# Four of the Mamba layer's x blocks formed by seven block products, with the convolution moved behind a round trip through DRAM

## The chip, the core and the metric

The kernel runs on one core of a Trainium2 chip. The metric is device microseconds of one execution, the median of three runs. The chip's engines are named as in the profile: PE (matrix products), PEld (its weight loads), DVE (vector), ACT (scalar), POOL (general purpose) and SP, which here issues DMAs.

## The reference

Two layers of a decoder over 256 tokens of width 2048 in float32: a latent attention mixer with a squared-ReLU MLP, then a Mamba-2 mixer with another MLP. Only the Mamba mixer changes:

```python
zxbcdt = h @ w_in                      # 2048 -> 4096 (z) + 4096 (x) + 1024 (b) + 1024 (c) + 64 (dt)
z, xbc, dt = jnp.split(zxbcdt, [SSM_D_INNER, SSM_D_INNER + SSM_CONV_DIM], axis=-1)
xbc = jax.nn.silu(causal_depthwise_conv(xbc, conv_w, conv_b))      # 4 taps along the tokens
xs, b_in, c_in = jnp.split(xbc, [SSM_D_INNER, SSM_D_INNER + SSM_GROUPS * SSM_STATE], axis=-1)
...
dt = jax.nn.softplus(dt.astype(jnp.float32) + dt_bias.astype(jnp.float32))
...
y = ssd_chunked_scan(xs, dt, a, b_in, c_in)    # one chunk of 256 tokens, 64 heads in 8 groups
y = y + d_skip * xs
y = y.reshape(B, S, SSM_D_INNER) * jax.nn.silu(z)
y = group_rms_norm(y) * norm_g                 # written out in the reference
return y @ w_out
```

## The kernel before

**Products.** Every float32 operand is split into a rounded part (`wh`, on ACT, L102) and the rest (`wl`, on DVE, L103). A product is three matmuls: rounded by rounded, rest by rounded, rounded by rest. Weights come in *units* of 128 partitions by 1024 floats (512 KB): two slices of depth 128 by 512 output columns. A plain unit is 12 matmuls (2 slices, 2 halves of the tokens, 3 each). `Flow` holds one fixed list of units for the whole run. `next` hands PE the unit at hand, has the splits of the next three put into the program, and the loads of up to six more. `raw` has 6 buffers, `wh` and `wl` 4 each, so a split can be at most four units ahead of PE.

**Order.** PE runs in the order in which the program is written. The other engines are ordered when the kernel is built: among what is ready, the earlier written comes first. After each key of a `block` (two units, 24 matmuls) `tick` is called, a *step*; `later(n, fn)` writes out `fn` at the step after n more. `pump` writes one or two heads of the scan per step. `behind("last_load")` and its like set an instruction behind the last load, split or `wh` written so far.

**The Mamba stage.** `SSM_ORDER` (L1408) names the blocks of 512 columns: B0, d (dt), C0, x0, B1, x1, C1, x2, z0 and so on, then the output blocks o0 to o3. What surrounds the change:

- `bc_block`: four keys, then `conv` in two halves, one step apart: PE transposes, 12 operations of DVE over a few columns each (L1122), tanh, and a last product (L1125).
- `dt_block`: one narrow product (L358), at a later step `fold` (L366) and `dt_chain`, some 20 small DVE operations that mostly wait on one another (L1151 to L1167); three steps later `cums` (L1173) on PE, one step later `back`.
- `x_block`: four keys, ACT copies the two results into `xt` (L1223) and writes them to DRAM (`xD`). Two steps later `shift` reads three shifted copies back (`taps`, L1231) on SP's queue. Then DVE does the four taps: `mult` (L1238, 3072 columns), `some` (L1241, L1243), `total` (L1247); ACT the tanh, DVE `silu` (L1254). `ahead` puts the group's eight heads into `pump`'s list and starts `across` (L1268).
- `head`: `cm` by DMA, four small ACT operations, a score product on DVE for four heads (L1306); after eight heads `products` (L1318) on PE.
- `z_block`: four keys, the gate once the group is ready (L1357 to L1363), transposes two steps later. `o_block`s follow when their groups are gated.

**Seven products in the MLP.** The MLP already forms pairs of 512-column blocks by a Winograd form of Strassen's scheme. The operand is cut in two by tokens and in two by depth, the weights in two by depth and in two by columns. `seven` (L170) gives the seven weight combinations, named M1, N7, N5, N6, N4, M2, N3, each in four depths d, and each a unit that PE uses for one half of the tokens only (6 matmuls). N7, N5 and N6 need an addition on DVE (L183) before their split, N4 an accumulating DMA from POOL (L199) after N6. `combinations` forms the token sums once (L528 to L538), and a planner, `merged`, weaves the units with plain ones so that DVE's work stays near a set share of PE's time.

## Time and profile before

| | us |
|---|---|
| median of 3 runs | 2287.03 (2286.62 to 2288.36) |
| the profiled execution | 2286.11 |
| its span, first to last instruction | 2284.3 |
| first matmul of B0 | 948.53 into the span |
| last output pair of the stage begins its second half (o3) | 1561.38 |
| the second MLP's first matmul | 1607.26 |

The profile is of one execution. In a view of groups a row gives line, engine, operation, output and input, shape and count, then busy time and mean ns of one, then the idle time of the engine just ahead of them. A row of waits reads: who waited for whom, total us, times, longest. The mean of one instruction includes its overlap with the next; distances between starts tell what a run of them costs.

### The profile page before, as it was taken

The numbers are of one execution on the slowest core, as the hardware profiler recorded it, in microseconds if no ns is written. First come the engines' busy times: TensorE is split into PE (matmuls) and PEld (weight loads), VectorE is DVE, ScalarE is ACT, GpSimd is POOL, SyncE is SP. The second block draws the span as 40 slices with busy tenths as digits, with TensorE's granted clock in tenths as the row PEclk, the third lists the DMA queues.
The fourth block names the chain that finished last, engine by engine and source line by source line (L and its number), as shares of the span: only waits on it lengthen the run. The fifth ranks groups of instructions, "written<-read, shape, count | busy, mean of one in ns | idle before, by whom it ended". The sixth has DMA issues, their size and how long they took to land.

```text
span 2284.3 us, 30685 instructions
## 1 busy us (share of the span) xinstructions
PE 2277.1 (100%) x10929; PEld 1889.3 (83%) x10929; DVE 1895.8 (83%) x2167; ACT 1407.8 (62%) x2006; POOL 268.0 (12%) x315
## 2 busy tenths in 40 slices
PE   9999999999999999999999999999999999999999
PEld 7898888888888888888888888888888888888887
DVE  7786697999898897677888678666989889989985
ACT  6775475666566666575666655545666666666663
POOL 1440000000000000100133212111000000000000
PEclk9999999999999999999999999999999999999999
DMA  8545678888888878667888878767688888888874
GB/s 315 173 153 153 215 229 263 260 259 271 263 253 260 270 231 271 228 191 262 275 278 280 254 255 279 228 217 228 205 259 250 263 269 254 259 275 249 265 233 160
DMA packets 167705, 557.16 MB, mean 244 GB/s; under 512 B 19040, under 2 KB 28192, under 8 KB 166528
## 3 DMA queue, kind: packets, MB, share of 16 engines
q1 hardware_dynamic: 151264, 502.44, 66.7%
q0 software_dynamic: 13888, 48.49, 10.1%
q10 hardware_dynamic: 2400, 4.27, 0.5%
q8 instruction: 86, 1.41, 0.2%
q14 instruction: 67, 0.55, 0.1%
HBM read 529.65 MB, written 6.41 MB: 235 GB/s over the span
## 4 chain that ended last, share of the span: by engine, by line
PE 97%; DMA 1%; DVE 1%; ACT 1%; issue 0%; POOL 0%; SPq 0%; ACTq 0%; DVEq 0%
PE acc L339 13%; PE acc L340 13%; PE acc L343 13%; PE yp L616 9%; PE yp L617 9%; PE yp L618 9%; PE st L617 7%; PE st L618 7%; PE st L616 7%; PE sm L324 1%; PE y L1318 1%; PE sm L322 1%; PE acc L617 1%; PE acc L618 1%; PE acc L616 1%; DMA wraw<-mi 1%
## 5 line engine op out<-in xcount | busy, mean ns | idle before, releaser
L102 ACT ACTIVATE wh<-wraw 128x1024 fp32r<-128x1024 f32 (+1 forms) x818 | 857.1, 1053 | 572.2 <-PE acc L340 263.0
L103 DVE TENSOR_TENSOR wl<-wraw,wh 128x1024 fp32r<-128x1024 f32 (+1 forms) x818 | 991.8, 1228 | 235.5 <-ACT wh L102 225.6
L616 PE MATMUL yp<-wh,k 128*128 128x512 f32 x896 | 349.2, 390 | 0.0
L618 PE MATMUL yp<-wh,k 128*128 128x512 f32 x896 | 348.8, 389 | 0.0
L617 PE MATMUL yp<-wl,k 128*128 128x512 f32 x896 | 348.6, 389 | 0.0
L339 PE MATMUL acc<-wh,xt 128*128 128x512 f32 x704 | 279.6, 397 | 1.1 <-ACT wh L102 1.1
L340 PE MATMUL acc<-wh,xt 128*128 128x512 f32 x704 | 274.6, 390 | 0.2 <-DVE xt L481 0.2
L102 ACT ACTIVATE wh<-wrx 128x1024 fp32r<-128x1024 f32 x168 | 177.8, 1059 | 152.8 <-PE yp L618 96.7
L103 DVE TENSOR_TENSOR wl<-wrx,wh 128x1024 fp32r<-128x1024 f32 x168 | 204.0, 1219 | 35.3 <-ACT wh L102 34.7
L618 PEld LDWEIGHTS yp<-wh,k 128*128 128x128 f32 x896 | 168.2, 188 | 35.2
L616 PEld LDWEIGHTS yp<-wh,k 128*128 128x128 f32 x896 | 168.2, 188 | 34.8
L617 PEld LDWEIGHTS yp<-wl,k 128*128 128x128 f32 x896 | 168.2, 188 | 34.8
L339 PE MATMUL acc<-wh,k 128*128 128x512 f32 x496 | 196.5, 396 | 0.0
L340 PE MATMUL acc<-wh,k 128*128 128x512 f32 x496 | 193.3, 390 | 0.0
L343 PE MATMUL acc<-wl,xt 128*128 128x512 f32 x704 | 188.3, 389 | 0.0
L616 PE MATMUL st<-wh,xt 128*128 128x512 f32 x448 | 177.7, 397 | 0.0
L618 PE MATMUL st<-wh,xt 128*128 128x512 f32 x448 | 174.9, 390 | 0.0
L617 PE MATMUL st<-wl,xt 128*128 128x512 f32 x448 | 174.7, 390 | 0.0
L339 PEld LDWEIGHTS acc<-wh,xt 128*128 128x128 f32 x704 | 132.4, 188 | 30.4 <-ACT wh L102 2.4
L340 PEld LDWEIGHTS acc<-wh,xt 128*128 128x128 f32 x704 | 132.3, 188 | 28.7 <-issue 1.2
L343 PEld LDWEIGHTS acc<-wl,xt 128*128 128x128 f32 x704 | 132.1, 188 | 27.7
L199 POOL DMA_DIRECT2D wrx<-mi x56 | 49.1, 876 | 719.8 <-DVE wl L103 523.7
(323 smaller groups left out, 3505.7 us busy)
## 6 DMA issues: line engine op xcount, KB each, us to landing
wraw<-mi SPq DMA_DIRECT2D x256, 512.0 KB, 5.5
wraw<-mo SPq DMA_DIRECT2D x256, 512.0 KB, 5.4
wraw<-si SPq DMA_DIRECT2D x160, 512.0 KB, 5.1
wraw<-so SPq DMA_DIRECT2D x64, 512.0 KB, 5.1
wrx<-mi SPq DMA_DIRECT2D x56, 512.0 KB, 5.2
wrx<-mi POOLq DMA_DIRECT2D x56, 512.0 KB, 7.6
wraw<-wo SPq DMA_DIRECT2D x32, 512.0 KB, 4.0
taps<-xD SPq DMA_DIRECT2D x16, 768.0 KB, 7.7
```

Source lines behind the costliest of these rows:

```text
L102: self.last = nc.scalar.activation(h[:, v], raw[:, v], AF.Copy)
L103: self.last_lo = nc.vector.tensor_tensor(lo[:, v], raw[:, v], h[:, v].bitcast(F32), ALU.subtract)
L199: nc.gpsimd.dma_start(st["b11"].tile, quarter(d, 1, 0), accum_op=ALU.add)
L322: self.nc.tensor.transpose(b.bitcast(F32R)[:, v], words[:, v], self.ident_r)
L324: self.nc.tensor.transpose(b[:, v], src[:, v], self.ident)
L339: nc.tensor.matmul(accs[t][:, :n], ah, wh[:, q, :], start=first and kt + q == 0, stop=False)
L340: nc.tensor.matmul(accs[t][:, :n], al, wh[:, q, :], start=False, stop=False)
L343: nc.tensor.matmul(accs[t][:, :n], lhs(kt + q, t)[0], wl[:, q, :], start=False, stop=en and q == nk - 1)
L616: nc.tensor.matmul(b, ah, wh, start=first and q == 0, stop=False)
L617: nc.tensor.matmul(b, ah, wl, start=False, stop=False)
L618: nc.tensor.matmul(b, al, wh, start=False, stop=last and q == 1)
L1318: nc.tensor.matmul(y[t][c, o], heads[j // 4][:, t, j % 4, c], xg[g][t][:, o], start=True, stop=True)
```

## The change

The x blocks 0 to 3 are taken out of the plain list and formed as two column pairs by seven products each. A first part runs B0, dt and the two pairs, each woven with two plain blocks (C0 and x4, then x5 and x6). All x results go to DRAM. A second part runs the remaining blocks, and in it `x_conv` (the steps `v0` to `v7`) reads x and its shifted copies back and does the convolution, then the heads as before.

The sums of tokens and the products:

```diff
+    def sums_of_tokens(self, pool):
...
+        def whole(i, t):
+            first = self.flow.pools["rx"] if len(f) < 3 else pool
+            v = first.tile([P, 1024], F32, tag="rx" if len(f) < 3 else "fy", name=self.name("xf"))
...
+            for q in range(2):
+                h, lo = (x[:, :, t * P:(t + 1) * P].bitcast(F32) for x in self.xT[2 * i + q])
+                nc.vector.tensor_tensor(v[:, q * 512:(q + 1) * 512].rearrange("p (k n) -> p k n", n=P), h, lo, ALU.add)
...
+        def one():
+            a21, a11, a22 = whole(0, 1), whole(0, 0), whole(1, 1)
+            sub(a22, a21, a22)
+            put("N5", a22)
...
+    def ssm_seven(self, S, p, filler, out):
...
+            elif name in ("N5", "N6"):
+                if count.get("N5") != 4 or count.get("N6") != 4:
+                    return
+                w, g, e = v["w"], v["g"], v["e"] = [self.scratch() for _ in range(3)]
+                sub(w, bank["N6"], v["m1"])
+                plus(g, bank["N7"], w)
+                plus(e, bank["N5"], g)
+                out(p, 1, 1, e, e)
...
+        for tok in woven(p):
+            if tok[0] != "s":
+                filler(tok)
+                continue
...
+                nc.tensor.matmul(bank[onto], ah, wh, start=done + q == 0 and not skip, stop=False, skip_group_check=skip)
+                nc.tensor.matmul(bank[onto], al, wh, start=False, stop=False, skip_group_check=skip)
+                nc.tensor.matmul(bank[onto], ah, wl, start=False, stop=done == 3 and q == 1, skip_group_check=skip)
+            if done == 3:
+                after(name)
+            self.spend(1.36)
+
+    def spend(self, us):
+        self.spent += us
+        if self.spent >= 5.4:
+            self.spent -= 5.4
+            self.tick()
```

M2 is summed onto M1's bank and N3 onto N5's. In the woven part a step comes when 5.4 us of planned PE time are spent. The convolution:

```diff
+        def put_x(g, t, src, dst):
+            nc.scalar.activation(dst, src, AF.Copy, scale=rs[t])
+            nc.scalar.dma_start(xD[3 + t * P:3 + (t + 1) * P, g * 512:g * 512 + 512], dst)
...
+        def x_conv(g):
+            xt = sp2.tile([P, 2, 512], F32, tag="xtm", name=f"xtm{g}", bufs=4)
...
+            def fetch():
                 with behind("last_load"):
...
+                    nc.sync.dma_start(xt, x_rows(g, 0, 2))
+                    weight(3)
+                    load(2)
+                    weight(2)
+                    load(1)
+                    weight(1)
+                    load(0)
...
+            def tapped(k):
+                nc.vector.tensor_tensor(tap[k], tap[k], both(k), ALU.mult)
+                nc.vector.tensor_tensor(xt, xt, tap[k], ALU.add)
...
             def mult():
...
                 with behind("last_lo"):
...
+                    nc.vector.tensor_tensor(xt, xt, both(3), ALU.mult)
+                    tapped(2)
+                with behind("last_load"):
+                    weight(0)
+                    weight(4)
...
+            self.later(0, fetch)
+            self.later(1, lambda: cb_group(g))
+            self.later(2, mult)
+            self.later(3, lambda: tapped(1))
+            self.later(4, total)
+            self.later(5, lambda: (silu(), ahead()))
```

`load(k)` reads 512 KB of rows shifted by k from `xD` into one of three `tap` tiles, `weight(k)` 256 KB of tap weights into one of three `cw` tiles. The two parts and their order:

```diff
+        with ExitStack() as first:
+            sp1 = first.enter_context(self.tc.tile_pool(name="ssm1", bufs=1, reuse_waits="tile"))
+            self.flow.pools["rx"] = first.enter_context(self.tc.tile_pool(name="rx", bufs=4, reuse_waits="tile"))
+            sums, steps = self.sums_of_tokens(sp1)
+            for n, fn in enumerate(steps):
+                self.later(n, fn)
+            bc_block("B", 0)
+            dt_block()
+            for p in range(2):
+                self.ssm_seven(sums, p, filler, lambda p, j, t, src, dst: put_x(2 * p + j, t, src, dst))
+        sp2 = later.enter_context(self.tc.tile_pool(name="ssm2", bufs=1, reuse_waits="tile"))
+        self.pump = pump
...
-SSM_ORDER = ["B0", "d0", "C0", "x0", "B1", "x1", "C1", "x2", "z0", "x3", "z1", "x4", "z2", "o0", "x5", "z3", "x6", "z4", "o1",
-             "x7", "z5", "z6", "o2a", "z7", "o2b", "o3"]
+SSM_FILLERS = [[("C", 0), ("x", 4)], [("x", 5), ("x", 6)]]
+SSM_ORDER = ["v0", "x7", "B1", "v1", "z0", "v2", "z1", "C1", "v3", "z2", "z3", "v4", "o0a", "v5", "o0b", "z4", "v6",
+             "o1a", "v7", "o1b", "z5", "z6", "o2a", "z7", "o2b", "o3"]
```

`woven(p)` lists the 28 block units and 16 plain units of a pair by a running count of planned PE and DVE time. Written out, the first pair begins C0.0, C0.1, M1, N7, C0.2, N5, C0.3, N6, C0.4, M1, N7, C0.5, C0.6, N5, C0.7 and ends M2 four times, N3 three times, N4, N3, x4.7. The second pair has the same form with x5 and x6. The banks of `conv` and `cb_group` now come from one pool of two (`sm`) alone, since the plain blocks of the woven part hold the other (`yp`). The head and score tiles lie in the second part's pool, the dt tiles in the first's.

## The prediction

> **What bounds the kernel now.** I read the page first: engines, chain, then the waits of PE, then the Mamba stage in windows.

> ```profile
> span 2284.3 us, 30685 instructions
> ...
> PE 2277.1 (100%) x10929; PEld 1889.3 (83%) x10929; DVE 1895.8 (83%) x2167; ACT 1407.8 (62%) x2006; POOL 268.0 (12%) x315
> PE 97%; DMA 1%; DVE 1%; ACT 1%; issue 0%; POOL 0%; SPq 0%; ACTq 0%; DVEq 0%
> ```

> PE is busy for the whole span and the chain that ended last is 97% PE. The waits of PE, complete:

> ```profile
> PE warmed L451 <- DVE warm L448: 1.4, 1, 1.4
> PE acc L339 <- ACT wh L102: 1.1, 1, 1.1
> PE yp L939 <- ACT xt L944: 0.6, 1, 0.6
> PE yp L939 <- DVE qn L887: 0.4, 1, 0.4
> PE acc L340 <- DVE xt L481: 0.2, 1, 0.2
> PE st L617 <- DVE wl L103: 0.2, 1, 0.2
> ```

> 3.9 us in all. So every matmul taken out shortens the run by its issue distance, and every new wait of PE lengthens it in full. The profiled execution took 2286.11 us, 1.8 over its span and 0.9 under the median of 2287.03; the sum is made on 2286.11 and the 0.9 added at the end.

> The windows' columns are stretch, length, then busy time (and instructions) of PE, PEld, DVE, ACT, POOL, then clock, DMA share, GB/s: nearly the whole Mamba stage, the middle of the second MLP, 150 us of x blocks, and 17 us that matter below.

> ```profile
> 950.50:1558.50 608.00, 608.00 (x3179) 501.26 (x3178) 465.81 (x510) 360.28 (x603) 115.66 (x75) 1.00 0.76 249
> 1629.00:2228.00 599.00, 598.83 (x2706) 494.22 (x2705) 545.33 (x533) 383.63 (x413) 37.49 (x52) 1.00 0.84 256
> 1110.00:1260.00 150.00, 150.00 (x888) 123.52 (x887) 131.49 (x128) 100.07 (x191) 52.20 (x29) 1.00 0.84 284
> 981.40:998.40 17.00, 17.00 (x80) 13.87 (x78) 15.52 (x34) 10.39 (x15) 0.00 (x0) 1.00 0.59 182
> ```

> The Mamba stage has DVE at 77% of PE's time, the MLP, which already forms its input product from seven block products, at 91%, both without a PE wait worth naming. The change spends DVE time to save PE time, so the question is whether DVE fits.

> **The saving.** Two ends of weight units on PE (a unit is 12 matmuls: eight with `wh`, four with `wl`):

> ```profile
> 921.10 1.07 PE L343 MATMUL acc<-wl,k 128*128 128x512 f32 x4
> 923.82 1.07 PE L343 MATMUL acc<-wl,k 128*128 128x512 f32 x4
> 887.01 0.40 PE L618 MATMUL st<-wh,xt 128*128 128x512 f32 x1
> 887.70 0.39 PE L618 MATMUL st<-wh,xt 128*128 128x512 f32 x1
> ```

> 923.82 - 921.10 = 2.72 us for 12, 0.227 each; in the MLP's block products three take 0.69, the same pace. Two plain x blocks are 2 x 8 units x 12 = 192 matmuls; seven products of four half units are 28 x 6 = 168. Two pairs save 2 x 24 x 0.227 = **10.9 us**. The transposes, score products and head products keep their counts, and `C0`, `x4`, `x5`, `x6` remain plain. The copies of x out of PSUM stay 16 on ACT; it issues 16 writes instead of 8, on an engine that is 62% busy.

> **What DVE gets.** First the prices: one 1024-column operation, its distance when they follow each other, and the small ones.

> ```profile
> L103 DVE TENSOR_TENSOR wl<-wraw,wh 128x1024 fp32r<-128x1024 f32 x231 | 276.9, 1219 | 26.3 <-ACT wh L102 22.4
> 1628.92 2.35 DVE L103 TENSOR_TENSOR wl<-wraw,wh 128x1024 fp32r<-128x1024 f32 x2
> 1631.19 1.22 DVE L103 TENSOR_TENSOR wl<-wrx,wh 128x1024 fp32r<-128x1024 f32 x1
> 1590.22 1.28 DVE L300 TENSOR_TENSOR xt<-sm,xt 128x512 fp32r<-128x512 f32 x2
> ```

> Alone 1.22, but two take 1631.19 - 1628.92 = 2.27 in sequence, so 1.14 each; for 512 columns two span 1.28 at 0.68 each, so they start 0.60 apart. A pair by seven products needs, for each of four depths, 2 operations for N7, N5, N6 and 1 for M1, N4, M2, N3: 40 instead of 16. That is 24 x 1.14 + 5 combinations x 0.60 = 30.3, twice 60.6. The sums of tokens add eight additions of 512 columns, four subtractions and four splits: 4.8 + 9.1 = 13.9. The convolution's one product of 3072 columns becomes three of 1024, the same elements, which I cost at nothing; two more starts per group would be under 2 us in all. DVE in the stage goes from 465.8 to 540.3 us, PE from 608 to 597: 90.5%, as in the MLP. On average it fits; by place it does not.

> **First part (B0, dt, two woven pairs).** PE needs 21.8 + 3.8 + 2 x 81.6 = 189 us. DVE: 2 x (56 x 1.14 + 3.0) = 134 for the pairs, 13.9, and 28 for B0, dt, the two halves of B0's and of C0's convolution and the residual: 176, 93%. But most of the extra lies in the first 50 us. The second MLP opens the same way, with its sums beside a plain block, and there DVE is only just in time:

> ```profile
> 1630.23 0.45 PE L617 MATMUL yp<-wl,xt 128*128 128x512 f32 x1
> ```

> The split that started at 1628.92 ended 1.2 us later, about 1630.1, and PE uses it at 1630.23: no lead is left. The Mamba stage adds B0's convolution and the dt chain at just that point. Before, the fold, the chain and the cumulative sums run so (rows of PE's and DVE's timelines, with others left out):

> ```profile
> 981.48 0.56 PE L366 MATMUL sm<-cst,s 128*128 128x64 f32 x4
> 983.62 0.27 DVE L1151 SCALAR_TENSOR_TENSOR dt<-sm,rs,cst 128x64 f32<-128x64 f32 x1
> ...
> 988.63 0.28 DVE L1158 TENSOR_TENSOR dt<-dt 128x128 f32<-128x128 f32 x1
> 988.83 1.22 DVE L103 TENSOR_TENSOR wl<-wraw,wh 128x1024 fp32r<-128x1024 f32 x1
> 990.57 0.22 DVE L1159 TENSOR_SCALAR dt<-dt 128x128 f32<-128x128 f32 x1
> 990.71 1.22 DVE L103 TENSOR_TENSOR wl<-wraw,wh 128x1024 fp32r<-128x1024 f32 x1
> ...
> 996.01 0.36 DVE L1166 SCALAR_TENSOR_TENSOR dt<-dt,aneg 128x64 f32<-128x64 f32 x2
> 998.39 0.65 PE L1173 MATMUL sm<-tri,dt 128*64 128x256 f32 x2
> ```

> The chain of small dependent operations takes 983.62 to 996.37 and is done 2.0 us before PE's fixed order reaches `cums` (L1173). After each dependent step a ready split slips in (L1158, L103, then L1159). In the change `cums` still comes three steps after the fold, 16.3 us of PE: M1, N7, C0.2, N5, C0.3, N6, C0.4, M1, N7. The window from fold to `cums` had DVE busy 15.5 of 17.0 with six splits (6.8 us); the nine units now need 13 operations, 14.8 us. 15.5 + 8.0 = 23.5, which is 6.5 over, and there is no lead to pay from. **PE waits 6.5 us, at `cums` or just ahead of it.** Bounds: were the chain preferred always, a lead of three units (about 4 us) could pay, 2.5; were each of some 15 dependent steps (0.3 us) followed by a 1.14 us operation, the chain takes 22 us after a start 2 us late, 24 against 16.9, plus ACT's part: up to 11. During this wait DVE runs its units ahead, so C0's convolution (6 us over two steps) is covered afterwards: the pairs alone use 67 of 81.6.

> The granted clock is 1.00 in every window above and PE never idles there. [...]

> **Second part (v0 to o3).** DVE has 540 - 176 = 364 us for 455 of PE. The last 26 steps (z5 to o3) hold 52 splits and little else, some 80 us; so the first 50 steps, with all eight convolutions, hold about 285 in 50 x 5.44 + 32 = 304 us: 94%. GpSimd makes DVE slower here:

> ```profile
> L103 DVE TENSOR_TENSOR wl<-wraw,wh 128x1024 fp32r<-128x1024 f32 x49 | 65.8, 1355 | 12.6 <-ACT wh L102 12.6
> wraw<-si SPq DMA_DIRECT2D x160, 512.0 KB, 5.1
> taps<-xD SPq DMA_DIRECT2D x16, 768.0 KB, 7.7
> cw<-cwx SPq DMA_DIRECT2D x8, 1280.0 KB, 8.7
> wrx<-mi POOLq DMA_DIRECT2D x56, 512.0 KB, 7.6
> ```

> (1355 ns in 1110 to 1260 against 1219 in the MLP; that is inside the 465.8.) DMA: 100 units x 0.524 MB, per group four times 0.524 and five times 0.262 MB instead of 1.57 + 1.31, and some 13 MB of head rows, gains and copies: 93 MB in 304 us, 306 GB/s. 284 GB/s took a share of 0.84, so 0.91. The rows read back were not seen in this form: 512 KB lies by size between 5 and 8 us (the first three rows), and `mult` comes two steps, 10.9 us, after `fetch`. They are hidden while the queue is free; without that cover DVE waits, and the 2.9 MB of one `fetch`, 9 us at 338 GB/s, also stand on SP's queue ahead of the next weights, which have some 16 us. SP issues six DMAs more per group. The new pool of this part lies where the sums lay, so the first `fetch` waits for PE's last N3, and x7's later weights stand behind it if SP gets there first. N6's eight accumulating DMAs on POOL land in 7.6 us by the last row, and N4 is planned 12 us after N6, so they are hidden as in the MLP; a late one would hold N4's split and what DVE has behind it. I take **2.5 us** of PE wait for this part, from 0 (like the MLP) to 12 (below).

> **Sum.** 2286.1 - 10.9 + 6.5 + 2.5 = 2284.2, with 0.9 for the median **2285.1 us**.

> **Rivals.** The measurement tells 0.2% (4.6 us) from no change.
> - *DVE keeps up* (32%): the chain is preferred (2.5) and the second part hides all: -8.4, 2278.6; with no loss at all 2276.1. For it: the MLP has 0.2 us of wait at 91%. Against it: the 6.5 over in a window without lead.
> - *DVE and DMA saturate in the second part* (24%): if DVE can be filled only to the MLP's 91%, 285 us of work take 313 instead of 304, +9, and with a few us of weights behind the read-backs +12: 2287.0 - 10.9 + 6.5 + 12 = 2294.6, slower. It decides from about 9 us in the second part. For it: 94% and a DMA share of 0.91, both above any window shown.
> [...]
> - That the change saves nothing has no room: 48 matmuls are gone from PE's list.

> **Chances.** Forecast 36% (2282.5 to 2291.5) and clock gate 8%, both within 0.2%: 44%. DVE keeps up: faster, 32%. Saturation: slower, 24%. The range takes in the first rival but for its last half us, and above it the saturated second part with 2.4 us more of the wait at `cums`, whose bound is 11: 2276.5 to 2297.

> **What would show it.** Right: a PE wait of 3 to 10 us at `cums` (or on a split just ahead) some 50 us after B0 starts, DVE without idle time from B0's start to there, the Mamba stage about 2 us shorter, PE waits in the second part under 5 us. Wrong: no PE wait at `cums` (then 2279), waits on splits spread over v1 to v6 (then 2290 and more), or a granted clock under 1 after a wait.

## The result and the profile after

| | before | after |
|---|---|---|
| median, us | 2286.82 (2286.37 to 2288.36) | 2346.03 (2342.47 to 2352.64, 4 runs) |
| after / before | | 1.0261, 95% interval 1.0237 to 1.0285 |
| span of the profiled execution, us | 2284.3 | 2345.2 |
| matmuls on PE | 10929 | 10881 |
| PE busy, us | 2277.1 | 2292.8 |
| PE not busy within the span, us | 7.2 | 52.4 |

The kernel is 59 us slower; the forecast was 2285.1 with a range to 2297. The page of the changed kernel, span, engines and the chain's shares:

```profile
span 2345.2 us, 30882 instructions
...
PE 2292.8 (98%) x10881; PEld 1895.2 (81%) x10881; DVE 1968.5 (84%) x2257; ACT 1439.3 (61%) x2036; POOL 269.1 (11%) x323
...
PE 33%; DMA 2%; DVE 2%; issue 1%; ACT 1%; SPq 0%; POOL 0%; DVEq 0%; ACTq 0%
```

The 48 matmuls are gone and DVE has 72.7 us more (74.5 were forecast). But the chain that ended last is no longer nearly all PE. The span's 60.9 us come apart in three terms: the saving, -10.9; PE not busy, 52.4 - 7.2 = +45.2; and PE busy for longer with fewer matmuls, 2292.8 - (2277.1 - 10.9) = +26.6. Together 60.9. The seven largest rows of PE's waits in the changed kernel (us in total, times, the longest):

```profile
PE sm L1302 <- DVE s L1225: 10.5, 2, 6.0
PE sm L322 <- DMA tr<-s: 6.6, 4, 4.0
PE sm L1277 <- DVE dt L1270: 6.3, 1, 6.3
PE sm L367 <- DVE s L1225: 4.4, 1, 4.4
PE sm L1216 <- DVE s L1225: 4.3, 1, 4.3
PE sm L1389 <- POOL s L1385: 3.9, 1, 3.9
PE acc L343 <- DVE wl L103: 3.1, 2, 2.0
```

`L1277` is `cums`: 6.3 us, where 6.5 were forecast. But it is one row of many. Three rows, 19.2 us, wait for a bank that `L1225` still reads (`L1302`, `L367`, `L1216`). The others wait for data: `cums` for dt, the transposes of `L322` for words that a DMA brings, `L1389` for a product of POOL. Waits on splits, which were the worry of the prediction, are 5.1 us: `L343` and, further down the list, `L618` with 2.0. In time, from PE's timeline (start, duration, operation, idle time before it and what ended it):

```profile
985.86 1.08 PE L367 MATMUL sm<-cst,s 128*128 128x64 f32 x4 [4.40 <-DVE s L1225]
1012.03 0.66 PE L1277 MATMUL sm<-tri,dt 128*64 128x256 f32 x1 [6.28 <-DVE dt L1270]
1037.41 0.44 PE L1216 MATMUL sm<-ident,s 128*128 128x128 f32 x1 [4.27 <-DVE s L1225]
1232.45 0.77 PE L1302 MATMUL sm<-k,k 128*128 128x256 f32 x1 [5.96 <-DVE s L1225]
1319.91 0.77 PE L1302 MATMUL sm<-k,k 128*128 128x256 f32 x1 [4.51 <-DVE s L1225]
```

Four of these five end when `L1225` ends: the tap operations of `conv`, which add up a half of B's or C's convolution straight out of the PSUM bank. DVE's timeline just ahead of the first of them:

```profile
977.13 0.47 DVE L1225 SCALAR_TENSOR_TENSOR s<-sm,cst,s 128x255 f32<-128x255 f32 x1
977.52 1.21 DVE L103 TENSOR_TENSOR wl<-wraw,wh 128x1024 fp32r<-128x1024 f32 x1
978.66 0.47 DVE L1225 SCALAR_TENSOR_TENSOR s<-sm,cst,s 128x254 f32<-128x254 f32 x1
979.05 1.21 DVE L103 TENSOR_TENSOR wl<-wraw,wh 128x1024 fp32r<-128x1024 f32 x1
980.18 0.47 DVE L1225 SCALAR_TENSOR_TENSOR s<-sm,cst,s 128x253 f32<-128x253 f32 x1
980.57 1.21 DVE L183 TENSOR_TENSOR wrx<-wrx,wraw 128x1024 f32<-128x1024 f32 x1
...
985.24 0.47 DVE L1225 SCALAR_TENSOR_TENSOR s<-sm,cst,s 128x253 f32<-128x253 f32 x1
```

Six operations of 0.47 us, in two chains of three that depend on one another, are 2.8 us of work. They take from 977.13 to 985.71, since a 1.2-us operation goes in after each. The fold (`L367`), next in line for a bank, begins at 985.86, just after the last has read it. PE runs in the order of the program, so everything behind the fold stands for those 4.40 us too. In the kernel before, the same half of B0 (there `L1122`) ran so:

```profile
976.81 1.51 DVE L1122 SCALAR_TENSOR_TENSOR s<-sm,cst,s 128x255 f32<-128x255 f32 x3
...
979.85 1.51 DVE L1122 SCALAR_TENSOR_TENSOR s<-sm,cst,s 128x255 f32<-128x255 f32 x3
```

Three at a time, with one split between the threes: 4.6 us instead of 8.6. And the next half worked on a bank of `yp`, so that `sm` had its second bank free.

The third term is mostly the clock. Windows of the same trace: in the first wait (981.46 to 985.86), from its last 0.8 us on, behind that, then behind a wait of 2.87 us (ended at 1384.82) and behind one of 2.01 us (ended at 1429.76). The column before the last two is the granted clock:

```profile
981.64:985.05 3.41, 0.00 (x0) 0.00 (x0) 3.06 (x5) 0.07 (x1) 0.00 (x0) 1.00 0.88 280
985.05:991.88 6.83, 6.02 (x16) 4.98 (x17) 5.52 (x12) 2.89 (x6) 0.00 (x0) 0.50 0.22 84
991.88:995.29 3.41, 3.41 (x16) 2.75 (x15) 2.79 (x7) 2.46 (x4) 0.00 (x0) 1.00 0.52 159
...
1384.90:1387.90 3.00, 3.00 (x10) 2.52 (x11) 3.00 (x3) 2.75 (x7) 0.00 (x0) 0.51 0.63 249
1429.80:1432.80 3.00, 2.90 (x17) 2.39 (x18) 3.00 (x3) 2.29 (x4) 0.00 (x0) 1.00 0.83 239
```

Behind the waits of 4.40 and 2.87 us the clock is 0.50 or 0.51, behind that of 2.01 us it is 1.00. At 0.50 PE has 16 matmuls in 6.02 us, at 1.00 16 in 3.41. From 987.28 to 991.55 they stand 0.43 us apart instead of 0.227. "Busy" hides this: PE is busy the whole time, only slower. The trace has ten such stretches in the Mamba stage, 54.6 us together, with PE busy for 45.6 of them; at half pace that is some 23 of the 26.6 us. The rest was not followed up.

### The profile page after: what moved, and what is told of

The parts are those of the page before. It is cut to its first block, busy times and chain, and to the rows that moved or that the text cites. A ratio compares the mean times of both kernels' runs of the same rounds, so it can differ in the third digit from the quotient of the medians.

```text
span 2345.2 us, 30882 instructions
## 1 busy us (share of the span) xinstructions
PE 2292.8 (98%) x10881; PEld 1895.2 (81%) x10881; DVE 1968.5 (84%) x2257; ACT 1439.3 (61%) x2036; POOL 269.1 (11%) x323
## 3 DMA queue, kind: packets, MB, share of 16 engines
q10 hardware_dynamic: 2528, 4.27, 0.5%
## 5 line engine op out<-in xcount | busy, mean ns | idle before, releaser
L102 ACT ACTIVATE wh<-wraw 128x1024 fp32r<-128x1024 f32 (+1 forms) x818 | 857.3, 1053 | 535.6 <-PE acc L340 197.6
L103 DVE TENSOR_TENSOR wl<-wraw,wh 128x1024 fp32r<-128x1024 f32 (+1 forms) x818 | 989.2, 1227 | 191.4 <-ACT wh L102 182.3
L617 PE MATMUL yp<-wh,k 128*128 128x512 f32 x896 | 349.3, 390 | 0.0
L618 PE MATMUL yp<-wl,k 128*128 128x512 f32 x896 | 348.6, 389 | 0.0
L102 ACT ACTIVATE wh<-wrx 128x1024 fp32r<-128x1024 f32 x192 | 203.3, 1059 | 177.0 <-PE yp L619 99.1
L103 DVE TENSOR_TENSOR wl<-wrx,wh 128x1024 fp32r<-128x1024 f32 x192 | 233.2, 1220 | 46.3 <-ACT wh L102 45.7
L339 PE MATMUL acc<-wh,k 128*128 128x512 f32 x496 | 197.0, 397 | 0.0
L617 PEld LDWEIGHTS yp<-wh,k 128*128 128x128 f32 x896 | 168.2, 188 | 34.9
L618 PEld LDWEIGHTS yp<-wl,k 128*128 128x128 f32 x896 | 168.2, 188 | 34.9
L340 PE MATMUL acc<-wh,k 128*128 128x512 f32 x496 | 193.9, 391 | 0.0
L339 PE MATMUL acc<-wh,xt 128*128 128x512 f32 x448 | 181.6, 405 | 0.0
L340 PE MATMUL acc<-wh,xt 128*128 128x512 f32 x448 | 178.2, 398 | 0.3 <-DVE xt L482 0.2
L617 PE MATMUL st<-wh,xt 128*128 128x512 f32 x448 | 177.7, 397 | 0.0
L618 PE MATMUL st<-wl,xt 128*128 128x512 f32 x448 | 174.7, 390 | 0.0
L618 PE MATMUL st<-wl,sN 128*128 128x512 f32 x336 | 131.6, 392 | 2.0 <-DVE wl L103 2.0
L617 PE MATMUL st<-wh,sN 128*128 128x512 f32 x336 | 133.1, 396 | 0.0
L343 PE MATMUL acc<-wl,k 128*128 128x512 f32 x496 | 132.7, 389 | 0.0
L619 PE MATMUL st<-wh,sN 128*128 128x512 f32 x336 | 131.1, 390 | 0.0
## 6 DMA issues: line engine op xcount, KB each, us to landing
wraw<-mi SPq DMA_DIRECT2D x256, 512.0 KB, 5.7
wraw<-mo SPq DMA_DIRECT2D x256, 512.0 KB, 5.5
wraw<-si SPq DMA_DIRECT2D x160, 512.0 KB, 5.5
wraw<-so SPq DMA_DIRECT2D x64, 512.0 KB, 5.2
wrx<-mi SPq DMA_DIRECT2D x56, 512.0 KB, 5.3
wrx<-mi POOLq DMA_DIRECT2D x56, 512.0 KB, 7.6
wraw<-wo SPq DMA_DIRECT2D x32, 512.0 KB, 3.9
tap<-xD SPq DMA_DIRECT2D x24, 512.0 KB, 6.8
```

What stands on the lines that cost most here:

```text
L102: self.last = nc.scalar.activation(h[:, v], raw[:, v], AF.Copy)
L103: self.last_lo = nc.vector.tensor_tensor(lo[:, v], raw[:, v], h[:, v].bitcast(F32), ALU.subtract)
L339: nc.tensor.matmul(accs[t][:, :n], ah, wh[:, q, :], start=first and kt + q == 0, stop=False)
L340: nc.tensor.matmul(accs[t][:, :n], al, wh[:, q, :], start=False, stop=False)
L343: nc.tensor.matmul(accs[t][:, :n], lhs(kt + q, t)[0], wl[:, q, :], start=False, stop=en and q == nk - 1)
L617: nc.tensor.matmul(b, ah, wh, start=first and q == 0, stop=False)
```

## The experiments

**Theory.** The time goes where PE, in order, needs one of two `sm` banks that a chain of dependent DVE operations still reads; the changed kernel's seven waits of 3 us and more (3.87 to 6.28) are each followed by half clock. **Rivals:** DVE is saturated and would be late anyhow; the loads queued on SP are late; the block products themselves cost it. Median, ratio to the kernel before on the same chip with its interval, and the two terms of each profiled execution above the kernel before (PE not busy; PE busy beyond what its matmuls took there):

| run | median us | ratio (95%) | not busy | busy beyond |
|---|---|---|---|---|
| after | 2346.03 | 1.0237-1.0285 | +45.2 | +26.6 |
| e1_copy | 2318.67 | 1.0122-1.0156 | +28.2 | +14.9 |
| e2_cums | 2340.15 | 1.0219-1.0250 | +42.9 | +21.9 |
| e3_cb | 2343.30 | 1.0218-1.0261 | +47.2 | +19.6 |
| e4_all | 2312.76 | 1.0096-1.0126 | +24.2 | +14.3 |
| e5_plain | 2325.07 | 1.0145-1.0182 | +24.3 | +16.5 |
| e6_notaps | 2316.71 | 1.0115-1.0153 | +28.9 | +12.5 |
| e7_pause (of before) | 2296.81 | 1.0028-1.0060 | see there | |
| e8_banks | 2315.57 | 1.0109-1.0145 | +27.3 | +11.8 |
| e9_ahead | 2314.09 | 1.0107-1.0137 | +28.9 | +14.2 |
| e10_all_notaps | 2301.60 | 1.0058-1.0092 | +15.2 | +8.1 |
| e11_plain_fix | 2310.55 | 1.0090-1.0121 | +15.0 | +7.2 |
| e12_pool | 2317.21 | 1.0124-1.0154 | +29.9 | +15.5 |
| e13_stage | 2314.19 | 1.0107-1.0141 | +22.0 | +15.0 |
| e14_spread | 2306.70 | 1.0073-1.0106 | +17.8 | +11.9 |
| e15_last | 2306.08 | 1.0071-1.0101 | +20.1 | +11.0 |
| e16_spread_banks | 2304.12 | 1.0064-1.0098 | +17.4 | +10.8 |
| e17_spread_banks_notaps | 2290.99 | 1.0013-1.0032 | +9.8 | +3.9 |

### e1_copy: the bank is emptied by one copy

```diff
-                a = self.scratch()
+                a, cp = self.scratch(), self.scratch()
+                nc.scalar.activation(cp, b, AF.Copy)
...
-                    s, o = b[:, k * 256:(k + 1) * 256], a[:, k * 256:(k + 1) * 256]
+                    s, o = cp[:, k * 256:(k + 1) * 256], a[:, k * 256:(k + 1) * 256]
...
-                th = self.scratch()
+                th = cp
```

> Each half of the convolution of B and C copies its PSUM bank to SBUF with one ACT operation, and ACT and DVE read the copy. Theory (banks): PE waits because its short products (fold, transposes, scores) need one of the two sm banks, which the convolution holds until six dependent DVE operations are done. The waits released by DVE L1225 (4.4 + 4.3 + 10.5 = 19.2 us) go, and with four waits gone some 2.6 us of half clock behind each: about 30 us less, 2316 us. Rival (DVE is full): PE waits as long, now for splits (L103) or elsewhere: within 8 us of the changed kernel's 2346.

2318.67, 27.4 us less (the theory said 2316), though ACT got eight copies more and DVE's work is the same. Waits of PE in this run:

```profile
PE acc L343 <- DVE wl L103: 6.0, 5, 1.8
PE sm L1390 <- POOL s L1386: 5.0, 2, 4.2
PE sm L322 <- ACT cb L1312: 4.7, 1, 4.7
```

No wait behind the tap operations is left; they were 19.2 us (10.5 + 4.4 + 4.3). The operations themselves are no faster on the copy (0.48 us on average in e4_all, which has this edit, and 0.48 in the changed kernel). So the held bank is the cause of nearly half of the loss, and a DVE that is just as full is no bar to that.

### e2_cums and e3_cb: two consumers come later

```diff
-            self.later(2, cums)
+            self.later(5, cums)
```

> The cumulative sums are written three steps later than in the changed kernel (six after the fold instead of three). Theory (fixed order): the dt chain is only late for its place in PE's order; the 6.3 us wait goes and with it about 2.6 us of half clock: 2337 us. Rival (DVE is full): the 6.3 us come back as waits for splits within the next 30 us: 2344 to 2348.

```diff
-            self.later(1, lambda: cb_group(g))
+            self.later(3, lambda: cb_group(g))
```

> The score products of a group are written three steps after the group's fetch step instead of one, so no longer in the same step as the second half of the convolution of B1 or C1. Theory (banks): the two waits of L1302 (10.5 us) go, with some 5 us of half clock: 2331 us; the third wait on a score bank (2.9 us at a transpose) may move. Rival (DVE is full): the waits move to splits or to the head products, 2341 to 2348.

2340.15, between e2's two expectations, and 2343.30, in the range of e3's rival. The wait that was aimed at goes, and another takes its place. First e2, then e3, from their waits of PE:

```profile
PE sm L1277 <- DVE s L1225: 5.4, 1, 5.4
```

```profile
PE acc L343 <- DVE wl L103: 11.9, 5, 5.9
PE sm L322 <- DMA tr<-s: 11.7, 3, 9.6
```

`cums` no longer waits for its data but for the bank that C0's half now holds; and in e3 the weights' splits and the transposes wait instead. The rival of e3, a wait that moves, was right.

### e4_all, e8_banks: together, and every bank emptied

e4_all is e1, e2 and e3 with `across` at lag 2. e8_banks adds to it a copy on ACT of the `cb` and `across` banks, on which DVE then works:

```diff
-            for o in (0, 256):
-                nc.vector.scalar_tensor_tensor(t[:, o:o + P], b[:, o:o + P], 0.125, tri[:, 0:P], ALU.mult, ALU.mult)
+            nc.scalar.activation(t, b[:, 0:384], AF.Copy, scale=0.125)
+            for o in (0, 256):
+                nc.vector.tensor_tensor(t[:, o:o + P], t[:, o:o + P], tri[:, 0:P], ALU.mult)
...
+                    nc.scalar.activation(far[g], b, AF.Copy)
-                    nc.vector.tensor_tensor(heads_of(far[g]), heads_of(b), spread(edge[:, 1]), ALU.mult)
+                    nc.vector.tensor_tensor(heads_of(far[g]), heads_of(far[g]), spread(edge[:, 1]), ALU.mult)
```

> All three edits, and the product across the halves of the tokens one step later. Theory (banks and fixed order): 19.2 + 6.3 + 3.9 us of waits go, with 7 or 8 spells of half clock at about 2.6 us: 2297 us, give or take 6. Rival (DVE is full): at least half of it comes back as waits for splits: above 2320 us.

> As the kernel with all edits (2312.8 us), and the score bank and the bank of the product across the halves are emptied by one ACT copy each, with DVE working on the copy. Theory (banks): the waits on score and far banks and those of L1303 (9.9 us) go, with some half clock: 2298 us, give or take 5. Rival (DVE and queues are full in the second part): PE waits as long for splits and copies: 2308 us or more.

e4_all came to 2312.76, between theory and rival; e8_banks to 2315.57, as its rival said. The first part is nearly healed in e4_all, as its window shows:

```profile
950.00:1010.00 60.00, 58.55 (x282) 48.55 (x281) 59.98 (x86) 37.16 (x49) 3.13 (x5) 1.00 0.66 208
```

DVE is busy 59.98 of 60 us and PE still 58.55. So a full DVE alone doesn't stop PE where no bank hangs on it. Most of what e4_all still loses lies behind 1140 us.

### e5_plain and e11_plain_fix: no products, the late convolution kept

```diff
-            for p in range(2):
-                self.ssm_seven(sums, p, filler, lambda p, j, t, src, dst: put_x(2 * p + j, t, src, dst))
+            for kind, i in SSM_PLAIN:
+                x_block(i) if kind == "x" else bc_block(kind, i)
...
+SSM_PLAIN = [("C", 0), ("x", 4), ("x", 0), ("x", 1), ("x", 5), ("x", 6), ("x", 2), ("x", 3)]
```

> The seven products alone are undone: x0 to x3 are plain blocks again, in a first part of B0, dt, C0, x4, x0, x1, x5, x6, x2, x3; the round trip through DRAM and the late convolution stay as in the changed kernel. Theory (each half of the change costs by itself): PE gets 10.9 us of matmuls back, the waits of the first part (16.7 us and three spells of half clock) go, those of the second part (26.9 us and six spells) stay: 2332 us. Rival (the products are all of the loss): 2290 us. Rival (the late convolution is all of it): 2350 us or more.

> e5_plain (no products, late convolution kept) with the bank of a convolution half copied, `cb_group` at lag 3 and `across` at lag 2. It tells what the late convolution costs once no bank is held. The second part is then that of e4_all: by the theory that the two halves of the change cost apart from each other, e4_all without its saving of 10.9 us and without its 3.5 us of waits in the first part: 2316 +-5, so that the products are worth 3 us or so when no bank is held by DVE. Rival, the second part is disturbed by what the first leaves behind (queues, weights not ahead): 2305 or less.

In this kernel x0 to x3 are plain blocks and the sums of tokens are left out. It takes 2325.07, 7 us less than its theory: the late convolution alone, with the new order and the narrower choice of banks that come with it, costs 38.7 us over the kernel before (2286.42 on that chip), and the products another 21 on top (2346.03 - 2325.07) where 10.9 of saving was due. With the banks of the convolution emptied and the two lags changed (e11) the late convolution alone still costs 24.5 (2310.55 against 2286.03; 2316 +-5 was expected). e4_all, which has the products too, stands 2.2 above e11, within the spread of both (some 5 us): freed of the banks, the products give back what they save.

### e6_notaps, e10_all_notaps: the second part with less DVE work

```diff
-                nc.vector.tensor_tensor(tap[k], tap[k], both(k), ALU.mult)
-                nc.vector.tensor_tensor(xt, xt, tap[k], ALU.add)
+                nc.vector.tensor_tensor(xt[:, :, 0:8], tap[k][:, :, 0:8], both(k)[:, :, 0:8], ALU.mult)
```

> The changed kernel without most of the convolution of x: each of the three shifted taps is one operation of 8 columns instead of two of 1024, so DVE has about 53 us less in the second part; all loads stay. Theory (a crowded DVE is what makes the small operations late in the second part): most of the second part's waits (26.9 us and their half clock, some 40 us) go: 2312 us, give or take 6. Rival (banks alone, whatever DVE's load): the waits on L1225 and on the score banks stay: 2330 us or more.

> e4_all and, in the second part, the DVE operations of the taps cut to 8 columns (the loads stay; so part of x's convolution is left out). Theory that what e4_all leaves is DVE's load in the second part, where a late split is a wait of PE: its 18 us of waits there and the half-clock time behind them go, the saving of 10.9 us shows, 2281 +-5. Rival, the loads (which stay) are what makes the second part late: 2300 or more.

e6 is that edit on the changed kernel, e10 on e4_all: 2316.71 and 2301.60. e6 came as expected. e10 did not reach 2281 and lies in the range of its rival, the loads (the next section). Its second part shows why "too much DVE work" can't be all of it. The same window of the kernel before, then of e10:

```profile
1140.00:1560.00 420.00, 420.00 (x2259) 346.05 (x2258) 323.22 (x321) 245.72 (x418) 104.22 (x67) 1.00 0.78 255
```

```profile
1140.00:1560.00 420.00, 408.85 (x2243) 334.99 (x2243) 299.62 (x368) 266.64 (x497) 90.61 (x72) 0.98 0.82 278
```

Before, DVE had 323 us in 420 and PE never stopped. In e10 it has 300, and PE stands for 11. In e4_all, with the taps, DVE has 349 and PE stands for 18: the load counts, but it does not decide alone.

### e9_ahead, e12_pool, e13_stage: the loads

e9 loads each head's row `cm` up to two steps early; e12 issues the taps' loads on GpSimd's queue; e13 issues each tap's load one step before its use. Each is made on e4_all; the core of e12:

```diff
-                nc.sync.dma_start(cw[k], d["cwx"][g][:, k * 512:(k + 1) * 512])
+                nc.gpsimd.dma_start(cw[k], d["cwx"][g][:, k * 512:(k + 1) * 512])
...
-                nc.sync.dma_start(tap[k], x_rows(g, 0, 2, k))
+                nc.gpsimd.dma_start(tap[k], x_rows(g, 0, 2, k))
```

> e4_all with the rows `cm` of a head loaded up to two steps before ACT reads them instead of in the same step. In e4_all ACT stands 44 us (15 times) at `mt` for `cm` in the second part, against 9.3 us (4 times) in the kernel before, and the `wh` copies of the next units are queued behind it. Theory that a good part of what e4_all still loses is this in-order wait on a load that the denser queue has made late: ACT's waits for `cm` fall under 10 us, the PE waits at L343 and L322 halve, 2300 +-6. Rival, DVE and the queue as a whole set the pace and ACT's wait only follows: 2308 or more, with the PE waits under other names.

> e4_all with the loads of the taps and their weights issued by GpSimd's queue instead of SP's. In e4_all SP stands 41 us in the second part at these loads (L1338, L1342) for DVE to free a buffer, and the loads of the next weights stand behind them in the same queue; in the kernel before it stood 9 us at such places. Theory that this queue is a good part of what e4_all still loses (26 us against the kernel before): these waits leave SP, the PE waits at L343 and L339 (7 us) go, 2303 +-5. Rival, DVE's load alone: 2309 to 2316. Third, GpSimd, whose own products now stand behind such waits, holds the outputs up: over 2318, with PE or DVE waits on POOL.

> e4_all with each tap's loads issued one step before their use, after the tap before it was used, instead of all at the fetch. SP no longer stands for DVE at the fetch (under 15 us instead of 41), but a load has one step of 5.4 us to land in 5 to 7 us. Theory of the queue: 2304 +-5, with DVE waiting on `cw` or `tap` more than the 12 us of e4_all. Rival, DVE's load alone or the loads' lateness takes the place: 2310 or more.

2314.09, 2317.21, 2314.19: none beats e4_all. e9 and e13 lie where their rivals put them, e12 between its rival (2316 at most) and its third way (over 2318). In e9 ACT still waited 37.9 us for `cm` from 1200 to 1560 us (e4_all: 44.2 from 1200 to 1550), so that edit did not do what it was to do, and its theory is untested rather than refuted. e12 says more. SP's waits of 1200 to 1560 us in e4_all, the same in e12, and PE's waits in e12:

```profile
SPq L85 <- DVE wl L103: 130.1, 72, 5.0
...
SPq L1338 <- DVE xtm L1362: 18.7, 6, 5.8
SPq L1338 <- DVE tap L1357: 17.9, 11, 4.3
```

```profile
SPq L85 <- DVE wl L103: 214.0, 100, 6.2
```

```profile
PE acc L343 <- DVE wl L103: 11.9, 8, 2.5
PE acc L339 <- DVE s L1468: 5.2, 1, 5.2
```

`L85` is the weights' load: an SP that waits there for a free tile is ahead of its consumers. With the taps' loads off its queue it waits 214 us, 84 more, so weights are early, and PE waits more all the same. So the weights' place behind these loads in SP's queue is not what e4_all loses by. That GpSimd, which now issues them, is held up instead is not excluded; nor do these runs say what the loads cost by their traffic.

### e14_spread, e15_last, e16 and e17: distance, and all together

e14 spreads the convolutions, nothing else (e15 moves only v5 and v7); e16 adds e8's two copies, e17 e10's cut.

```diff
-SSM_ORDER = ["v0", "x7", "B1", "v1", "z0", "v2", "z1", "C1", "v3", "z2", "z3", "v4", "o0a", "v5", "o0b", "z4", "v6",
-             "o1a", "v7", "o1b", "z5", "z6", "o2a", "z7", "o2b", "o3"]
+SSM_ORDER = ["v0", "x7", "B1", "v1", "z0", "z1", "v2", "C1", "v3", "z2", "z3", "v4", "o0a", "o0b", "v5", "z4", "o1a", "v6", "o1b", "z5", "v7", "z6", "o2a", "z7", "o2b", "o3"]
```

> e4_all with the convolutions of the last groups spread out: in SSM_ORDER v2 stands behind z1, and v5, v6 and v7 each stand one half or whole block later (o0b, z4, o1a ahead of v5 and v6; o1b and z5 ahead of v7). Nothing is left out and no operation is added. Theory that what e4_all still loses is DVE's load by place, some 5 us of it per 5.44-us step while eight convolutions stand in two thirds of the second part: with more steps between them the late splits are fewer, 2303 +-5. Rival, that the loss comes from each step's own order of dependent operations and not from the distance of the convolutions: 2309 to 2316. A third way: heads that come late leave a gap at the end of the stage, over 2318 with waits at z7 or o3.

> e4_all with only v5 and v7 of SSM_ORDER moved one half block later (v5 behind o0b, v7 behind o1b). The same theories in a smaller dose: if distance decides, a third to a half of what e14_spread gains, 2308 +-4; if not, 2313 +-3.

> e14_spread with the `cb` and `across` banks emptied by one copy on ACT, as in e8_banks. Of e14_spread's waits in the second part about 10 us (L322 behind `k`, `cb` and `far`) are waits for a bank that DVE or ACT still reads, and a half-clock time follows each. Theory that with the convolutions apart these waits no longer only move to the splits as they did in e8_banks: 2297 +-5. Rival, they move again: 2303 or more, with L343 and L339 waiting on `wl` and `wh`.

> e16_spread_banks and the taps' DVE operations cut to 8 columns (part of x's convolution left out). If held banks, distance and the taps on DVE are all that stands against the saving, then 2276 plus the first part's 3.5 us of waits, 2280 +-5. If more is in it (the loads, the read-back rows, ACT in order), 2290 or more.

e14 gains 6.1 and e15 6.7 us on e4_all: the order counts, with the same work, but the smaller dose did as much as the larger. e16 reaches 2304.12, which is where its rival put it (2303 or more, with `L343` waiting on splits: 8.5 us in the profile), not its theory (2297). It is the best version that computes everything; it is still 0.81% (0.64 to 0.98) behind the kernel before. e17 falls to 2290.99, in the range for "more is in it" (2290 or more). Its second part:

```profile
1140.00:1560.00 420.00, 415.18 (x2294) 340.36 (x2293) 308.55 (x372) 276.98 (x509) 94.67 (x70) 1.00 0.83 285
```

The saving is real: PE is busy for 2270.1 us, 7.0 less than in the kernel before. With 9.8 us of PE not busy and 3.9 of busy time beyond the matmuls left, e17's span is 2.8 above the kernel before (13.7 - 10.9). The 3.9 are not half clock: e17's granted clock is 1.00 in each of its windows, which reach to 2280 us. The steps down from the changed kernel, each measured on the one before: halves' banks 27.4 (e1), lags 5.9 (e4), distance 6.1 (e14), `cb` and `across` banks 2.6 (e16), the taps' DVE operations 13.1 (e17). Runs of one kernel spread over 2 to 12 us, and set against the kernel before on its own chip the step of e16 is 1.6, so the small steps are rough.

### e7_pause: what a pause costs by itself

Two pauses in the kernel before, near its end, each by a short chain that a transpose on PE must wait for; the second has three GpSimd operations in it.

```diff
+            if gain is None and nb in PAUSES:
+                b = self.bank(False)
+                nc.tensor.matmul(b, self.x[0][0][:, 0:P], self.x[0][0], start=True, stop=True)
+                t = self.scratch()
+                nc.scalar.activation(t, b, AF.Copy)
+                for _ in range(PAUSES[nb]):
+                    nc.gpsimd.tensor_tensor(t, t, t, ALU.mult)
+                b = self.bank(False)
+                nc.tensor.transpose(b[:, 0:P], t[:, 0:P], self.ident)
```

> The kernel before, with two pauses of PE near its end: after the first and the second of the last four output blocks PE does one extra product, ACT copies it, and a transpose of PE waits for the copy; in the second pause three operations of GpSimd come between. Nothing else waits there. Theory (half clock after a wait): the granted clock drops to 0.5 behind the long pause (some 6 us) for some 5 us, so the long pause costs about 2.6 us more than it lasts; the short one (about 1.5 us) costs at most 1 us more than it lasts. Rival (the clock in the records is an artefact of the trace): the time grows by the two pauses and the extra products alone.

PE's timeline at both pauses:

```profile
2249.74 0.33 PE L711 MATMUL sm<-ident,s 128*128 128x128 f32 x1 [0.69 <-ACT s L707]
...
2250.13 0.40 PE L340 MATMUL acc<-wh,k 128*128 128x512 f32 x1
2250.37 0.40 PE L339 MATMUL acc<-wh,k 128*128 128x512 f32 x1
...
2266.41 0.48 PE L711 MATMUL sm<-ident,s 128*128 128x128 f32 x1 [4.56 <-POOL s L709]
...
2267.11 0.63 PE L340 MATMUL acc<-wh,k 128*128 128x512 f32 x1
2267.54 0.63 PE L339 MATMUL acc<-wh,k 128*128 128x512 f32 x1
...
2272.57 0.39 PE L339 MATMUL acc<-wh,k 128*128 128x512 f32 x1
2272.79 0.39 PE L340 MATMUL acc<-wh,k 128*128 128x512 f32 x1
```

The pauses came out shorter than expected (0.69 and 4.56 us for 1.5 and 6). After 0.69 us of pause the matmuls keep 0.23 us; after 4.56 us they stand mostly 0.43 apart from 2266.54 to 2272.23, 5.7 us for 13 matmuls that take 3.0 at full pace: 2.7 us lost. Pauses and lower pace make 4.56 + 0.69 + 2.7 = 8.0 of the span's 10.5 us more; the six matmuls added take 2.2 (2248.03 to 2249.82 and 2260.83 to 2266.54, without the waits), which leaves 0.3. The granted clock is 0.50 from 2266.40 to 2270.00. So the lower pace behind the pause of 4.56 us needs none of the changed kernel's surroundings.

## Why the prediction was wrong

Against the saving the sum set 6.5 + 2.5 = 9.0 us of PE waits, and nothing for the clock. The profile shows 45.2 us more of PE not busy and 26.6 more of busy time. Three steps failed: "covered afterwards" in the first part, the 2.5 us of the second part, and the clock at nothing.

**The saving: right.** 48 matmuls are gone at the pace that was reckoned with, and in e17, where most waits are gone, PE's busy time is 7.0 us lower.

**What DVE gets: right.** 72.7 measured for 74.5. e5, with the moved convolution and no products, has 0.3 us of DVE more than the kernel before (1896.1 against 1895.8), so the convolution's change was rightly put at nothing. DVE is busy 60.0 of the 63.5 us from B0's start to `cums`.

**The wait at `cums`: right in place and cause, and in size partly by luck.** 6.28 for 6.5; one operation of the weights goes in after most steps of the dt chain. But from fold to `cums` PE worked 19.9 us, not 17.0, since it ran at half clock for part of it, and the chain took 26.1 us, not 23.5, since DVE was busy for only 23.0 of them. The two misses cancel. And the step "the pairs alone use 67 of 81.6", by which C0's convolution was to be "covered afterwards", failed: PE waits 4.27 us at its transposes (`L1216`), and 4.40 at the fold before `cums`. Neither was in the sum. The cover was reckoned in DVE time. What failed is that the operations don't only have to be done somewhere: until the last of six is done they hold one of two banks, and PE, in order, can't go past the next matmul that needs one. Before the change the same operations held their bank for half as long, and the banks came in turn from both pools; the section on the result shows both. The chain's stretching was seen for dt, and not asked of the other chains.

**The second part: wrong by the most.** 2.5 us were taken, 12 as the bound; PE's waits there come to 27 us in the profile, with half clock behind many of them. The bound was one of DVE's load ("94%"), and load alone is not what decides: in e10 PE stands for 11 us with less DVE work than the kernel before had. Half of the 27 us (10.5 at `L1302`, 2.9 at `L322` behind `cb`) are waits for a bank, which the bound did not look at; the rest are waits for a DMA, for POOL and for splits. The 94% itself came out of two slips: the 364 us of DVE end at 1558.5 and the 455 of PE at the end of the stage, where the kernel before has 35.6 us of DVE more, and the last 151 us of the stage hold 110 us of DVE there, not 80. The two nearly cancel (400 - 110 = 290 for 285).

**The rival of a saturated DVE and queue: right in its sign only.** It gave 2294.6 by 12 us. In e4_all a DVE at 59.98 of 60 us lets PE go on, and in e12 the weights are early again without gain. Banks, order and the taps' operations on DVE each take a part (27.4, 6.1 and 13.1 us in the steps above); none of them is all of it.

**The clock: a term that should have been part of the forecast.** The sum has nothing for it, and the 8% that the chances give a clock gate were the author's estimate: no trace that was there to read shows such a drop. That the granted clock is 1.00 in the windows of the kernel before was no evidence against one, since PE's longest wait in that trace is 1.4 us. What the runs showed in its place: behind `cums` PE works 3.74 us at half clock, so it loses some 1.9. There are ten such stretches in the changed kernel's Mamba stage, of 3.41 or 6.83 us each, and they make most of the 26.6 us. The clock is 0.50 in them and 1.00 again behind them. A wait of 2.87 us is followed by one, and so are two short ones of 1.25 and 1.24 us (the last section).

**The test named beforehand decided rightly:** "waits on splits spread over v1 to v6" and "a granted clock under 1 after a wait" were both to show it wrong. The spread is there; but the waits are for banks, and in the second part for a DMA and for POOL, more than for splits.

**Open.** e17 leaves 13.7 us, of which PE's idle time in its second part is 4.8 and in the first some 3.4. Why the taps' operations cost 13 us in e16, when DVE has idle time in the same 420 us, was not settled: the distance of the convolutions is part of it (e14), the order within a step was not tried alone. What the 3.9 us of busy time in e17 are was not followed up either. More buffers for the taps, and a third `sm` bank, weren't tried. The version that keeps the products but convolves at once, as before, wasn't tried either.

## What to carry to other kernels

Where PE works in a fixed order, list for each PSUM bank what must finish before it is free, and how much of an engine's other work can slip between those operations; an engine's total load doesn't show this, and one copy out of the bank can be worth more than all the work it adds (eight ACT copies for 27.4 us here). A wait of PE can cost more than its length. In the changed kernel one or two stretches of 3.41 us at half clock followed each wait of 2.87 us and more (an estimate, half of 3.41: up to 1.7 us lost in each); behind e7's pause of 4.56 us 2.7 us were lost. A saving of 11 us on the bounding engine that lengthens chains on another needs all such chains looked at, not only the one with the least lead.

## What the chip showed that was not expected

```profile
1284.45 0.50 PE L322 MATMUL sm<-ident,tr 128*128 128x128 f32 x4 [1.25 <-DMA tr<-s]
1286.19 0.59 PE L322 MATMUL sm<-ident,tr 128*128 128x128 f32 x3 [1.24 <-DMA tr<-s]
```

```profile
1286.30:1289.30 3.00, 3.00 (x10) 2.50 (x11) 3.00 (x4) 1.54 (x2) 0.00 (x0) 0.50 0.87 265
```

- The changed kernel's runs spread over 10 us (2342.47 to 2352.64), those of the kernel before over 2. That small shifts of its loads decide which waits grow would fit this, but was not tested.
